# Order of the scan's parameters, the adaLN blocks, the routing groups and the final norm's scalings in a hybrid decoder block

## The chip, the cores and the metric

The kernel runs on one core of a Trainium2 chip. The metric is the device time of one execution in microseconds, as the median of several runs. The engines are TensorE (PE: matmul and transposes), VectorE (DVE), ScalarE (ACT), GpSimd (POOL) and SyncE (SP, which here only issues transfers); each runs its own instructions in program order and waits for the others at semaphores. Sixteen DMA engines move data for all of them.

## What is computed

One layer of a decoder block on x of 1024 tokens by 1024 channels, all float32, batch 1. Cut to what matters:

```python
sh1, sc1, gt1, sh2, sc2, gt2 = jnp.split(silu(c) @ w_ada + b_ada, 6, axis=-1)
xn = modulate(rmsnorm(h, norm1_g), sh1, sc1)
z_a, z_u, z_v = columns of xn @ w_in
y_a = s5_branch(z_a, ...)         # 32 groups x 64 complex states, diagonal scan over the tokens, GLU
y_b = sgu_branch(z_u, z_v, ...)   # gating with 128 x 128 causal mixing
g_a, g_b = halves of sigmoid(xn @ w_gate + b_gate)
h = h + gt1 * ((g_a * (y_a @ w_branch_a) + g_b * (y_b @ w_branch_b)) @ w_out)
xn2 = modulate(rmsnorm(h, norm2_g), sh2, sc2)
h = h + gt2 * hierarchical_moe(xn2, ...)   # top 1 of 4 groups, then top 2 of its 8 SwiGLU experts
return rmsnorm(h, norm_f_g)
```

The scan needs, for each of its 32 x 64 states, exp, cosine and sine of the parameters, powers of them, and from these tables of 128 x 128. Each token goes to two of 32 experts; each expert has two weights of 1024 x 512 and one of 512 x 1024, 201 MB in all.

## The kernel before

Tokens lie in eight tiles of 128 (NJ = 8), channels in eight blocks of 128 (KD = 8). A float32 product is made of three matmuls on split operands, high by high, low by high, high by low (`mm3`, L112 to L114).

**Prologue, to 33 us.** ScalarE squares the eight tiles of x and sums them (`square`, L558), VectorE makes the reciprocal roots of four tiles at a time (`norm_scale(h)`) and scales them, TensorE transposes them by halves of four tiles (`norm_turn(h, act)`, L572; copies out by ScalarE, or half by VectorE). `mod_block(b)` sums a quarter of the conditioning projection on TensorE (L586), copies the sums on ScalarE (`wide`), transposes them (L592) and adds the bias on VectorE. `xn_block(b)` applies shift and scale to two channel blocks and splits them. Then come the z_a products of four token tiles, two channel blocks at a time, with `xn_block(b + 1)` and `mod_block(b + 2)` between them.

`ssm_setup` is a generator that makes the scan's parameters, mostly on GpSimd with 128x16 operands; each `next(setup)` runs it to its next `yield`. Its inputs pass through three small transposes on TensorE (`prow`, L361) and one copy on ScalarE (`par`). Its rest goes to a list of side generators, of which one step is taken for each unit of products that TensorE is given. The products of the token mixer follow, unit by unit, with the transposes of the scan's tables (L524, L545) at fixed units.

**Out-projection and routing, some 560 to 668 us.** For each token tile j there are two units (j, n) of 24 matmuls each. After unit (j, 1) the tile's norm, its transposes (L1355), its router product (L1372, sixteen matmuls), its scaled row `x2` for the experts (two ScalarE instructions and two GpSimd additions, then a store to `xrows`) follow. For two tiles at a time (GROUPS) `route` picks groups and experts on VectorE (tile `rt`), counts on TensorE (L1464 to L1467), makes one-hot rows on VectorE (`ohr`), moves them on TensorE (L1493) and scatters them to a table on GpSimd (L1507). `WAIT` says for a group after how many units its two TensorE steps are put; a group not in it has (1, 1). The scatter of the last group is put off to a list `late_rows`, which runs after the first gathers.

**Experts, 668 to 1207 us.** The experts' rows are gathered by GpSimd (`x_fetch`, L1675), TensorE transposes them (L1690) and multiplies; results are added to rows in memory by GpSimd (`y_add`, L1725). Some experts have large slots with split weights, the others small slots of 64 rows. The weights are loaded on SyncE's queue into two pools of buffers; `load_next` issues the next load of a fixed list after a given expert's step. `DRAINS` names six experts after which GpSimd gets a drain instruction. Within this part, `gf_steps` spreads the final norm's gain over the partitions.

**Tail, from some 1205 us.** Eight tiles of the result are loaded. ScalarE squares each (`sum_sq`), VectorE makes the roots for three at a time (`scales(j, n)`), multiplies each tile by root and gain (`put`), and SyncE stores it. The rows of the last expert (`hlate`) are made apart, by two 64x512 instructions, and scattered by GpSimd after all stores.

## Time and profile before

| what | value |
|---|---|
| median of three runs | 1239.01 us (1237.97 to 1239.11) |
| profiled execution | 1239.78 us |
| its span | 1238.1 us |
| mean granted clock of TensorE | 0.965 |
| busy: TensorE, VectorE, ScalarE, GpSimd | 92%, 59%, 37%, 30% of the span |

The span is the part of the execution that the profiler's records cover. A clock of 1 is 2.4 GHz and 0.5 is 1.2 GHz; a mean in between says how the stretch divides into the two. Busy shares are means over stretches with different limits, so each stretch is read for itself: first which engine is busy all the time, then what the waits of that engine end on. An instruction row gives its start, its duration (of all its repetitions together where it says x4), engine, line, what it writes and reads, and in brackets how long its engine was idle before it and what ended that.

### The profile page before, as it was taken

Reading aid. Unit: us, or ns where it says so; the run is one execution under the profiler, and the core shown is the slowest. Engines: PE = TensorE matmul, PEld = TensorE weight load, DVE = VectorE, ACT = ScalarE, POOL = GpSimd, SP = SyncE. Lnnn points to the kernel's source line nnn. Section 1 sums busy time; section 2 is a strip of 40 time slices with the busy share of each in tenths; the row PEclk is TensorE's granted clock in tenths of the full one; section 3 lists DMA queues with packets and bytes.
Section 4 is the critical chain, followed back from the end, with each engine's and each line's share of the span. In section 5 each row is a group of like instructions: output and inputs, shape, how many; then the busy total and the mean of one; then the engine's idle time right before and its main releaser. Section 6 shows DMA issues by size and latency. Waiting matters only on the chain. (4 is left out here: it accounts for less than half of the span.)

```text
span 1238.1 us, 16769 instructions
## 1 busy us (share of the span) xinstructions
PE 1133.7 (92%) x6237; PEld 872.7 (70%) x6238; DVE 735.2 (59%) x1223; ACT 463.2 (37%) x664; POOL 377.6 (30%) x477
## 2 busy tenths in 40 slices
PE   4998999999999999999995999999898999898980
PEld 4897888888878888788774776666565666665630
DVE  4614562568597555656668976666464566565616
ACT  6422233234215421034324754444342444443303
POOL 2799273533000211415565111111111111111210
PEclk9999999999999999999897999999899998999995
DMA  9711122583541155545466999999999999998986
GB/s 333 222 35 58 62 86 57 197 289 102 190 151 52 35 190 175 185 166 219 152 229 241 339 353 396 401 402 404 406 400 404 388 397 377 380 394 310 381 301 271
DMA packets 106663, 313.44 MB, mean 253 GB/s; under 512 B 21035, under 2 KB 59527, under 8 KB 91858
## 3 DMA queue, kind: packets, MB, share of 16 engines
q1 hardware_dynamic: 92520, 274.14, 58.6%
q0 software_dynamic: 9088, 20.32, 6.3%
q10 hardware_dynamic: 4970, 17.88, 3.7%
q8 instruction: 50, 0.82, 0.3%
q14 instruction: 35, 0.29, 0.1%
HBM read 287.02 MB, written 33.83 MB: 259 GB/s over the span
## 5 line engine op out<-in xcount | busy, mean ns | idle before, releaser
L87 DVE TENSOR_TENSOR ewl<-wexp,ewh 128x1024 fp32r<-128x1024 f32 x176 | 207.8, 1221 | 82.0 <-ACT ewh L108 79.8
L108 ACT ACTIVATE ewh<-wexp 128x1024 fp32r<-128x1024 f32 x176 | 174.3, 1053 | 38.8 <-DMA wexp<-in_w 36.3
L112 PE MATMUL mm<-xn,wh 128*128 128x512 f32 x320 | 127.4, 398 | 0.0
L114 PE MATMUL mm<-xn,wl 128*128 128x512 f32 x320 | 125.1, 391 | 0.0
L113 PE MATMUL mm<-xn,wh 128*128 128x512 f32 x320 | 125.0, 391 | 0.0
L87 DVE TENSOR_TENSOR wl<-wraw,wh 128x1024 fp32r<-128x1024 f32 x38 | 55.0, 1456 | 110.5 <-ACT wh L108 110.5
L1741 PE MATMUL mm<-wexp,xs 128*64 128x256 f32 x992 | 115.4, 382 | 3.9 <-DMA wexp<-in_w 3.6
L1675 POOL DMA_INDIRECT xg<-xrows,w x29 | 30.7, 1060 | 282.8 <-PE aux L1690 128.6
L113 PE MATMUL mm<-ewl,xth 128*128 128x512 f32 x256 | 103.2, 403 | 0.7 <-DVE ewl L87 0.7
L1741 PEld LDWEIGHTS mm<-wexp,xs 128*64 128x64 f32 x992 | 69.0, 137 | 48.9 <-issue 9.1
L112 PE MATMUL mm<-ewh,xth 128*128 128x512 f32 x256 | 102.3, 400 | 0.2 <-ACT xth L108 0.2
L114 PE MATMUL mm<-ewh,xtl 128*128 128x512 f32 x256 | 100.5, 393 | 0.0
L1725 POOL DMA_INDIRECT hbuf<-yo,w x28 | 52.8, 1887 | 123.1 <-DVE yo L87 109.7
L798 ACT ACTIVATE gate<-mm,vcol 128x512 f32<-128x512 f32 x32 | 22.0, 688 | 134.7 <-PE mm L114 134.7
L112 PE MATMUL mm<-ewh,w 128*128 128x512 f32 x128 | 55.9, 437 | 17.7 <-ACT ewh L108 17.7
L112 PEld LDWEIGHTS mm<-xn,wh 128*128 128x128 f32 x320 | 60.4, 189 | 13.7 <-issue 1.6
L114 PEld LDWEIGHTS mm<-xn,wl 128*128 128x128 f32 x320 | 60.2, 188 | 12.8
L113 PEld LDWEIGHTS mm<-xn,wh 128*128 128x128 f32 x320 | 60.4, 189 | 11.8
L87 DVE TENSOR_TENSOR yo<-mm,macc 128x512 f32<-128x512 f32 (+1 forms) x64 | 42.7, 686 | 41.6 <-PE mm L1741 37.5
L108 ACT ACTIVATE w<-aux 128x512 fp32r<-128x512 f32 x16 | 9.6, 597 | 140.5 <-PE aux L1709 140.5
L113 PEld LDWEIGHTS mm<-ewl,xth 128*128 128x128 f32 x256 | 48.3, 189 | 19.3 <-DVE ewl L87 10.1
L108 ACT ACTIVATE wh<-wraw 128x1024 fp32r<-128x1024 f32 x38 | 39.6, 1052 | 58.6 <-PE mm L113 29.6
(369 smaller groups left out, 2454.1 us busy)
## 6 DMA issues: line engine op xcount, KB each, us to landing
wexp<-in_w SPq DMA_DIRECT2D x76, 2048.0 KB, 25.5
wexp<-in_w SPq DMA_DIRECT2D x48, 512.0 KB, 12.0
wadr<-in_w_ada SPq DMA_DIRECT2D x32, 512.0 KB, 4.8
wexq<-in_w SPq DMA_DIRECT2D x24, 512.0 KB, 9.1
wada<-in_w_ada SPq DMA_DIRECT2D x8, 1024.0 KB, 11.2
wraw<-in_w_gate SPq DMA_DIRECT2D x16, 512.0 KB, 3.8
gate<-gate ACTq DMA_DIRECT2D x16, 512.0 KB, 2.8
gin<-gate SPq DMA_DIRECT2D x16, 512.0 KB, 3.8
```

Of the source, the lines that this page charges most:

```text
L87: eng.tensor_tensor(out=o, in0=a, in1=b, op=op)
L108: A.activation(out=hi, in_=raw, func=AF.Copy)
L112: T.matmul(out=ps, lhsT=lh, rhs=rh, start=first, stop=False)
L113: T.matmul(out=ps, lhsT=lh, rhs=rl, start=False, stop=False)
L114: T.matmul(out=ps, lhsT=ll, rhs=rh, start=False, stop=last)
L798: A.activation(out=box["g"][:, sl], in_=box[hf], func=AF.Sigmoid, bias=col("bg", 8 * s + d))
L1675: G.indirect_dma_start(out=xg, out_offset=None, in_=rows[:, :], in_offset=bass.IndirectOffsetOnAxis(ap=xi, axis=0), bounds_check=rows.shap ...
L1725: G.indirect_dma_start(out=rows[:, :], out_offset=bass.IndirectOffsetOnAxis(ap=yi, axis=0), in_=yo, in_offset=None, bounds_check=rows.shap ...
L1741: T.matmul(out=ps[sl, 0:n], lhsT=xt[:, k, HALF * h:HALF * (h + 1)], rhs=w[:, n * g:n * (g + 1)], start=(kt == 0), stop=(kt == nk - 1), til ...
```

## The change

It has seven places.

1. `ssm_setup` yields once more, at step 2, and `next(setup)` is called earlier: twice before the squares, once between `norm_scale(0)` and the eighth square, once after half 0's transposes, and once more at the end.
2. `norm_turn` takes the channel blocks that it transposes. `mod_block` is cut into `mod_sums` and `mod_cols`. `norm_turn(1, ...)` is spread around the first block's two parts, and the second block's `mod_block` and `xn_block` come after the first 48 matmuls of z_a. `wz[0].split()` comes earlier.
3. `WAIT` is {(2, 3): (2, 2), (4, 5): (2, 3)} instead of {(4, 5): (2, 2), (6,): (4, 2)}, and the scatters of group (4, 5) go to `late_rows` too.
4. The last tile's row `x2` is made by one VectorE instruction.
5. The loads after a large expert's step are written two steps earlier.
6. `DRAINS` names two experts instead of six, and `gf_steps` makes a second form of the gain (`gh`) by two GpSimd copies.
7. In the tail two tiles are finished by VectorE as before; the other six are multiplied by the gain on VectorE (`by_g`) and by the root on ScalarE (`put_scaled`). The roots are made for two, three, three and one; `hlate` takes one 128x512 instruction.

```diff
@@ -565,8 +565,8 @@
         for j in range(4 * h, 4 * h + 4):
             ts(xt[j], xt[j], rs1[:, j:j + 1], None)
-    def norm_turn(h, act):
-        for k in range(KD):
+    def norm_turn(h, ks, act):
+        for k in ks:
             ps = ps_aux()
             for i in range(4):
                 T.transpose(ps[:, i * P:(i + 1) * P], xt[4 * h + i][:, k * P:(k + 1) * P], ident)
@@ -577,24 +577,30 @@
                 act_copy(o, ps)
-    mcs = {}
-    def mod_block(b):
+    mcs, mrows = {}, {}
+    def mod_sums(b):
         mps = ps_aux()
         for k in range(KD):
             for q in range(4):
                 T.matmul(out=mps[32 * q:32 * q + 32, 0:P], lhsT=cact[:, k:k + 1].to_broadcast([P, 32]),
                          rhs=wa[b][:, k, q // 2, (q % 2) * P:(q % 2 + 1) * P],
                          start=(k == 0), stop=(k == KD - 1), tile_position=(0, 32 * q))
-        mrow = tmp("wide", [P, P], bufs=1)
-        act_copy(mrow, mps[:, 0:P])
+        mrows[b] = tmp("wide", [P, P], bufs=1)
+        act_copy(mrows[b], mps[:, 0:P])
+    def mod_cols(b):
         tps = ps_aux()
-        T.transpose(tps[:, 0:P], mrow, ident)
+        T.transpose(tps[:, 0:P], mrows[b], ident)
         mc = mcs[b] = tmp("mc", [P, 4], bufs=4)
         mcv = mc.rearrange("p (s i) -> p s i", s=2)
         tt(mcv, tps[:, 0:P].rearrange("p (s i z) -> p s i z", s=2, i=2)[:, :, :, 0],
            col("b1", 0, 16).rearrange("p (s k) -> p s k", s=2)[:, :, 2 * b:2 * b + 2], OP.add)
         stt(mc[:, 2:4], mc[:, 2:4], 1.0, col("g1", 2 * b, 2), OP.add, OP.mult)
+    def mod_block(b):
+        mod_sums(b)
+        mod_cols(b)
     xn = {}
@@ -630,7 +636,7 @@
     def ssm_setup():
         for i, _ in enumerate(ssm_params()):
-            if i in (0, 1) or i % 3 == 1:
+            if i in (0, 1, 2) or i % 3 == 1:
                 yield
         first = build_tables(0)
         for _ in range(3):
@@ -651,32 +657,46 @@
     NA = 4
     setup = ssm_setup()
-    for j in range(NJ):
+    next(setup)
+    next(setup)
+    for j in range(NJ - 1):
         square(j)
     norm_scale(0)
+    next(setup)
+    square(NJ - 1)
     norm_scale(1)
+    norm_turn(0, range(KD), True)
     next(setup)
-    norm_turn(0, True)
-    norm_turn(1, False)
-    mod_block(0)
     wz[0].split()
-    next(setup)
+    mod_sums(0)
+    norm_turn(1, range(2), True)
+    mod_cols(0)
+    norm_turn(1, range(2, 4), True)
     xn_block(0)
-    mod_block(1)
+    norm_turn(1, range(4, KD), False)
     wz[2].load()
     wz[3].load()
     load_ssm()
     acc = [ps_mm() for _ in range(NA)]
     for b in range(4):
-        next(setup)
-        if b < 3:
+        if 0 < b < 3:
             wz[b + 1].split()
             xn_block(b + 1)
+        if b:
+            next(setup)
         for i in range(2):
             for j in range(NA):
                 za_mm(acc[j], j, 2 * b + i)
+            if b == i == 0:
+                mod_block(1)
+                wz[1].split()
+                xn_block(1)
         if b < 2:
             mod_block(b + 2)
+    next(setup)
     for j in range(NA):
         za_read(j, acc[j])
     side.append(setup)
@@ -1241,7 +1261,7 @@
     LASTCUT = 12
-    DRAINS = (1, 7, 13, 19, 25, NEXP - 4)
+    DRAINS = (14, NEXP - 5)
     rest = []
     def w_load(nm, e, q=nc.sync, whole=True, later=None, small=False, key=None):
@@ -1370,10 +1390,14 @@
         lps = ps_aux()
         for k in range(KD):
             T.matmul(out=lps[:, 0:36], lhsT=ht[:, k], rhs=rk["wr"][:, k], start=(k == 0), stop=(k == KD - 1))
-        for hf in range(2):
-            hs = slice(hf * 512, (hf + 1) * 512)
-            A.activation(out=x2[:, hs], in_=x2[:, hs], func=AF.Identity, scale=r)
-            tt(x2[:, hs], x2[:, hs], rowv[3][:, hs], OP.add, G)
+        if j == NJ - 1:
+            stt(x2, x2, r, rowv[3], OP.mult, OP.add)
+        else:
+            for hf in range(2):
+                hs = slice(hf * 512, (hf + 1) * 512)
+                A.activation(out=x2[:, hs], in_=x2[:, hs], func=AF.Identity, scale=r)
+                tt(x2[:, hs], x2[:, hs], rowv[3][:, hs], OP.add, G)
         nc.scalar.dma_start(out=xrows[j * P:(j + 1) * P, :], in_=x2)
         if j == NJ - 1:
             load_next(nc.scalar, nc.gpsimd)
@@ -1386,7 +1410,7 @@
             yield from route(tiles, L)
     late_rows = []
-    WAIT = {(4, 5): (2, 2), (6,): (4, 2)}
+    WAIT = {(2, 3): (2, 2), (4, 5): (2, 3)}
     GROUPS = ((0, 1), (2, 3), (4, 5), (6, 7))
     def route(tiles, L):
@@ -1511,7 +1535,7 @@
                 scatters.append(ins_)
         for t in range(B):
             tt(cum, cum, mb[:, t], OP.add)
-        if tiles[-1] >= NJ - 2:
+        if tiles[-1] >= NJ - 4:
             late_rows.append(scatter)
         else:
             scatter()
@@ -1658,6 +1682,12 @@
             T.matmul(out=ps, lhsT=rk["onef"], rhs=hi[:, hs], start=True, stop=False)
             T.matmul(out=ps, lhsT=rk["onef"], rhs=lo[:, hs], start=False, stop=True)
             act_copy(g[:, hs], ps)
+        gh = k4("gfh", [DM])[:, 0:512]
+        gf.append(gh)
+        for h in range(2):
+            sl = slice(HALF * h, HALF * (h + 1))
+            G.tensor_copy(out=gh[sl], in_=g[sl, 512 * h:512 * (h + 1)])
         yield
     late = gf_steps()
@@ -1841,6 +1871,12 @@
             hts_[e] = hid_turn(hidt, *htp)
         else:
             hid_turn_s(hid_s, xsr[1][:, e % 2])
+    def next_loads(at):
+        for _ in loads_after.get(at // 4, []):
+            load_next()
     def after(at, nm, e, i):
@@ -1881,9 +1917,8 @@
                 G.drain()
         if at < 4:
             next(ranks, None)
-        if i == 3:
-            for _ in loads_after.get(at // 4, []):
-                load_next()
+        if i == 3 and not is_l(e):
+            next_loads(at)
         if (nm, e, i) == ("w2", NEXP - 3, 0):
             late_tiles()
         if (nm, e, i) == ("w1", NEXP - 1, 0):
@@ -1907,6 +1942,8 @@
     ranks = ranking()
     for at, (nm, e, i) in enumerate(stream):
         split_to(at, at + AHEAD)
+        if is_l(e) and i == 4 - AHEAD:
+            next_loads(at)
         if nm == "w2":
             if i == 0:
                 yps[e] = [ps_mm(), ps_mm()] if is_l(e) else ps_mm()
@@ -1941,33 +1978,56 @@
         yield
         yield from rsqrt_steps(frs[:, sl], fsq[:, sl], n)
+    def store(j):
+        nc.sync.dma_start(out=out[j * P:(j + 1) * P, :], in_=hx[j])
     def put(j):
         stt(hx[j], hx[j], frs[:, j:j + 1], gf[0], OP.mult, OP.mult)
-        nc.sync.dma_start(out=out[j * P:(j + 1) * P, :], in_=hx[j])
+        store(j)
+    byg = {0: xgs[0], 1: xgs[1]}
+    def by_g(j):
+        tt(byg.setdefault(j, hx[j]), hx[j], gf[0], OP.mult)
+    def put_scaled(j):
+        A.activation(out=hx[j], in_=byg[j], func=AF.Identity, scale=frs[:, j:j + 1])
+        store(j)
     def run(steps):
         for _ in steps:
             pass
+    for j in range(4):
+        sum_sq(j)
+    by_g(0)
+    by_g(1)
+    run(scales(0, 2))
+    put_scaled(0)
+    by_g(2)
+    by_g(3)
+    sum_sq(4)
+    put_scaled(1)
+    sum_sq(5)
+    run(scales(2, 3))
+    put(4)
+    put_scaled(2)
     tt(lt["h"], lt["h"], yos[NEXP - 1][:, 0:512], OP.add)
-    for j in range(NJ):
-        sum_sq(j)
+    sum_sq(6)
+    sum_sq(7)
+    by_g(5)
+    by_g(6)
     A.activation(out=dump[:, 0:512], in_=lt["h"], func=AF.Square, accum_out=fsq[:, NJ:NJ + 1])
     sps = ps_aux()
     T.matmul(out=sps[:, 0:1], lhsT=lt["both"], rhs=fsq[:, NJ:NJ + 1], start=True, stop=True)
-    run(scales(0, 3))
-    for j in range(3):
-        put(j)
-    run(scales(3, 3))
-    for j in range(3, 6):
-        put(j)
-    V.tensor_copy(out=fsq[:, NJ:NJ + 1], in_=sps[:, 0:1])
-    run(scales(6, 3))
-    put(6)
+    put_scaled(3)
+    run(scales(5, 3))
+    put_scaled(5)
     put(7)
-    for g in range(2):
-        sl = slice(HALF * g, HALF * (g + 1))
-        stt(lt["h"][sl], lt["h"][sl], frs[sl, NJ:NJ + 1], gf[0][sl, 512 * g:512 * (g + 1)], OP.mult, OP.mult)
+    put_scaled(6)
+    run(scales(NJ, 1, sps[:, 0:1]))
+    stt(lt["h"], lt["h"], frs[:, NJ:NJ + 1], gf[1], OP.mult, OP.mult)
     G.indirect_dma_start(out=out_h[:, :], out_offset=bass.IndirectOffsetOnAxis(ap=x_index(NEXP - 1), axis=0), in_=lt["h"],
                          in_offset=None, bounds_check=2 * NT - 1, oob_is_err=False)
```

**ScalarE in the prologue.** Before, the end of the squares and of the transposes' copies (`aux_301` is half 1's seventh block) reads as follows; `wide` are the sums of an adaLN block, `wh` the high part of a weight, `xn` the split input, `par` the scan's parameters:

```order
L105 ACTIVATE xht_137<-aux_301 128x512
L105 ACTIVATE wide_346<-aux_313 128x128
L108 ACTIVATE wh_353<-wraw_109 128x1024
L615 ACTIVATE xn_68_383<-xht_131,mc_350 128x1024
L615 ACTIVATE xn_68_383<-xht_132,mc_350 128x1024
L105 ACTIVATE wide_424<-aux_391 128x128
L105 ACTIVATE par<-aux_448 128x48
L108 ACTIVATE wh_493<-wraw_114 128x1024
L615 ACTIVATE xn_68_383<-xht_133,mc_428 128x1024
L615 ACTIVATE xn_68_383<-xht_134,mc_428 128x1024
```

After the change the copy of `par` stands between the squares of the seventh and the eighth tile:

```order
L558 ACTIVATE sqs_199,ssq_129<-x_96 128x1024
L558 ACTIVATE sqs_201,ssq_129<-x_97 128x1024
L105 ACTIVATE par<-aux_223 128x48
L558 ACTIVATE sqs_229,ssq_129<-x_98 128x1024
L105 ACTIVATE xht_131<-aux_250 128x512
```

and half 1's copies (`xht`) stand between the first block's parts, with the second `wide` behind the first `xn` (L621 was L615):

```order
L108 ACTIVATE wh_337<-wraw_109 128x1024
L105 ACTIVATE wide_374<-aux_341 128x128
L105 ACTIVATE xht_131<-aux_376 128x512
L105 ACTIVATE xht_132<-aux_382 128x512
L105 ACTIVATE xht_133<-aux_393 128x512
L105 ACTIVATE xht_134<-aux_399 128x512
L621 ACTIVATE xn_65_405<-xht_131,mc_390 128x1024
L621 ACTIVATE xn_65_405<-xht_132,mc_390 128x1024
L105 ACTIVATE xht_135<-aux_413 128x512
L105 ACTIVATE xht_137<-aux_425 128x512
L105 ACTIVATE wide_498<-aux_465 128x128
L108 ACTIVATE wh_505<-wraw_114 128x1024
```

What moved: `par` forward by eighteen places, and half 1's copies behind the first `wide`.

**TensorE behind tile 5's products.** Before, the counting group of (2, 3) follows the last product of unit (5, 1) (`mm_5104`); `rt_4968` is that group's routing tile:

```order
L113 MATMUL mm_5104<-wo_4432,mh_4838 128x512
L114 MATMUL mm_5104<-wo_4431,ml_4839 128x512
L1464 LDWEIGHTS before
L1464 MATMUL aux_5143<-rt_4968,before 128x32
L1467 LDWEIGHTS ones
L1467 MATMUL aux_5143<-cum,ones 128x32
```

and the rest of that group stands ahead of tile 4's router product (L1372) and the first product of tile 6:

```order
L1467 LDWEIGHTS ones
L1467 MATMUL aux_5143<-cum,ones 128x32
L1372 MATMUL aux_5171<-rk_2032,ht_4942 128x36 x8
L1355 MATMUL aux_5185<-ident,h_4842 128x128 x4
L112 MATMUL mm_5204<-wo_4100,mh_5005 128x512
```

After, the router product (now L1392) and the transposes (now L1375) follow tile 5's products directly:

```order
L113 MATMUL mm_5104<-wo_4432,mh_4838 128x512
L114 MATMUL mm_5104<-wo_4431,ml_4839 128x512
L1392 MATMUL aux_5141<-rk_2032,ht_4942 128x36 x8
L1375 MATMUL aux_5155<-ident,h_4842 128x128 x4
L112 MATMUL mm_5174<-wo_4100,mh_5005 128x512
```

and the counting group (now L1488 and L1491) stands behind twelve products of tile 6:

```order
L114 MATMUL mm_5174<-wo_4100,ml_5006 128x512
L1488 LDWEIGHTS before
L1488 MATMUL aux_5189<-rt_4968,before 128x32
L1491 LDWEIGHTS ones
L1491 MATMUL aux_5189<-cum,ones 128x32
```

The group moved behind the router product and twelve products of other work.

**ScalarE in the tail.** Before, the eight squares, of which the order prints four and four, and that of `hlate` are the last work:

```order
L1700 ACTIVATE w_747_5610<-mm_9072 128x256
L105 ACTIVATE hts_6031<-aux_9121 128x256
L1936 ACTIVATE dump_9136,nrm<-tail_9077 128x1024 x4
L1936 ACTIVATE dump_9136,nrm<-tail_9078 128x1024 x4
L1955 ACTIVATE dump_9136,nrm<-hlate_9034 128x512
```

After, scalings (L1995) stand among the squares (L1973); the rows begin with that of tile 1, the second of three ahead of the last tile's square:

```order
L1995 ACTIVATE tail_9073<-xg_5603,nrm 128x1024
L1973 ACTIVATE dump_9132,nrm<-tail_9074 128x1024
L1995 ACTIVATE tail_9073<-tail_9073,nrm 128x1024
L1973 ACTIVATE dump_9132,nrm<-tail_9074 128x1024 x2
L2021 ACTIVATE dump_9132,nrm<-hlate_9030 128x512
L1995 ACTIVATE tail_9073<-tail_9073,nrm 128x1024
L1995 ACTIVATE tail_9074<-tail_9074,nrm 128x1024 x2
```

Three scalings now stand ahead of the last tile's square, and three behind the square of `hlate`.

## Rows read from the trace of the kernel before

**Rows 1.** Stretches: us, busy us (instructions) of each engine, clock, DMA share, GB/s

```profile
core 0: us, PE busy (x) PEld busy (x) DVE busy (x) ACT busy (x) POOL busy (x), PEclk, DMA share, GB/s
600.00:640.00 40.00, 35.05 (x187) 29.71 (x185) 33.14 (x134) 10.67 (x24) 20.27 (x22) 0.91 0.57 194
640.00:680.00 40.00, 26.56 (x125) 21.13 (x124) 27.23 (x94) 16.31 (x26) 22.12 (x23) 0.75 0.70 256
760.00:1120.00 360.00, 338.60 (x1788) 231.65 (x1788) 218.40 (x235) 156.85 (x193) 65.35 (x44) 0.97 1.01 396
```

**Rows 2.** TensorE's waits: us in total, times, longest

```profile
PE aux L545 <- DVE w L90: 4.4, 1, 4.4
PE aux L524 <- DVE sbr L87: 1.1, 1, 1.1
```

**Rows 3.** TensorE's timeline, 103 to 110 us: start, duration, line, tiles

```profile
103.59 1.97 PE L545 MATMUL aux<-ident,w 128*128 128x128 f32 x8 [4.35 <-DVE w L90]
...
105.79 0.63 PE L113 MATMUL mm<-xn,wh 128*128 128x512 f32 x1
106.21 0.63 PE L114 MATMUL mm<-xn,wl 128*128 128x512 f32 x1
...
109.11 0.39 PE L113 MATMUL mm<-xn,wh 128*128 128x512 f32 x1
109.34 0.39 PE L114 MATMUL mm<-xn,wl 128*128 128x512 f32 x1
```

**Rows 4.** GpSimd's timeline, 33 to 42 us

```profile
33.05 0.66 POOL L94 TENSOR_SCALAR par<-par 128x16 f32<-128x16 f32 x1 [18.95 <-ACT par L105]
...
39.61 1.14 POOL L87 TENSOR_TENSOR sp<-sp 128x16 f32<-128x16 f32 x1
...
41.18 0.22 POOL L87 TENSOR_TENSOR sp<-sp 128x16 f32<-128x16 f32 x1
```

**Rows 5.** Timeline of ScalarE, then of TensorE, ahead of the first products

```profile
16.88 1.06 ACT L558 ACTIVATE sqs<-x 128x1024 f32<-128x1024 f32 x1 [0.62 <-DMA x<-in_x]
...
32.11 0.33 PE L592 MATMUL aux<-ident,wide 128*128 128x128 f32 x1 [1.19 <-ACT wide L105]
```

**Rows 6.** TensorE's timeline, 605 to 642 us, around the routing groups

```profile
608.44 0.18 PE L1464 MATMUL aux<-rt,before 128*128 128x32 bf16 x1 [2.62 <-DVE rt L87]
...
608.57 3.46 PE L1372 MATMUL aux<-rk,ht 128*128 128x36 f32 x16
...
620.83 1.42 PE L1372 MATMUL aux<-rk,ht 128*128 128x36 f32 x12
...
637.93 1.43 PE L1493 MATMUL aux<-ohr 128*128 128x64 f32 x8 [1.57 <-DVE ohr L94]
...
640.36 0.63 PE L112 MATMUL mm<-wo,mh 128*128 128x512 f32 x1
```

**Rows 7.** VectorE's timeline: the same three routing steps of three groups

```profile
605.97 0.42 DVE L87 TENSOR_TENSOR rt<-rt 128x8 f32<-128x8 f32 x3
...
624.01 4.26 DVE L87 TENSOR_TENSOR rt<-rt 128x8 f32<-128x8 f32 x1
...
654.30 1.20 DVE L87 TENSOR_TENSOR rt<-rt 128x8 f32<-128x8 f32 x3
```

**Rows 8.** GpSimd's timeline, late scatters and expert 3's gather

```profile
672.82 0.99 POOL L1507 DMA_INDIRECT table<-rk,rt  x1 [0.30 <-issue]
...
683.02 1.04 POOL L1675 DMA_INDIRECT xg<-xrows,w  x1 [6.87 <-PE aux L1690]
```

**Rows 9.** Timelines of ScalarE, VectorE and GpSimd in the tail

```profile
1218.59 1.06 ACT L1936 ACTIVATE dump<-tail 128x1024 f32<-128x1024 f32 x1 [0.88 <-DMA tail<-hbuf]
...
1221.17 3.68 DVE L90 SCALAR_TENSOR_TENSOR tail<-tail,nrm,gf 128x1024 f32<-128x1024 f32 x3
...
1227.25 2.48 DVE L90 SCALAR_TENSOR_TENSOR tail<-tail,nrm,gf 128x1024 f32<-128x1024 f32 x2
...
1233.40 1.03 POOL L1971 DMA_INDIRECT out<-hlate,w  x1 [26.47 <-SPq L1978]
```

## The prediction

> **What bounds the kernel now.** I read the table of stretches first, then TensorE's waits, then the timelines around each wait. In the table [rows 1] the reader is to see three kinds of stretch. Up to 600 us the waits of TensorE, below, are the exceptions; from 600 to 680 it is busy for only 35.05 and 26.56 of 40 us, at a granted clock of 0.91 and 0.75, with DMA at 0.57 and 0.70; from 760 to 1120 DMA stands at 1.01 with 396 GB/s, while TensorE has 338.60 of 360 us. So a microsecond saved ahead of 680 is worth something only if the experts' weight loads start earlier too. They do so far as the profile tells: with DMA at 0.57 and 0.70 between 600 and 680 the loads there wait for buffers, which TensorE and VectorE free, and those events move forward with the products. After 1200 the tail is a chain of its own.
>
> **Scan parameters first.** TensorE waits once 4.4 us for the table `w` of the scan and once 1.1 us for `sbr` [rows 2]. After the 4.35 us the eight transposes take 1.97 us [rows 3]; the following products stand 0.42 us apart (105.79 to 106.21) and four of them pass before the spacing is 0.23 again (109.11 to 109.34): four times 0.2, 0.8 us. At full clock I take the transposes at half, about 1.0 us. So the place costs 4.35 + 1.1 + 1.0 + 0.8 = 7.2 us. The tables are late because GpSimd's chain of parameters begins only at 33.05, after 18.95 us of idling for `par` [rows 4]. The change puts the three transposes of `prow` first on TensorE and the copy of `par` on ScalarE ahead of the eighth square, where ScalarE sits 0.62 us for the last tile of x [rows 5] and the copy is a 128x48 tile. GpSimd then starts at about 16.5, that is 16.5 us earlier; the tables are also asked for one unit earlier (some 5.5 us by the spacing of 24 products of 0.23 us). 16.5 - 5.5 leaves 11 us against a lateness of 4.35, so both waits should vanish: **7.2 us**, all on TensorE's path. Bounds: 0 if something else on that chain is late (the rival below), 7.2 otherwise.
>
> What can slow this chain is VectorE: GpSimd's product of 128x16 takes 1.14 us at 39.61 and 0.22 us at 41.18 [rows 4], the long one beside VectorE's 128x1024 products. In its new place it runs beside the scaling of x and a chain of fourteen tiny VectorE instructions. The Trainium skill ("SBUF — State Buffer", section "Who interferes with whom") calls the port pair of VectorE and GpSimd an exclusive lock that a loser waits out for a whole instruction; it speaks against this edit, since by it the fourteen could each wait for one 0.22 us instruction, 3 us in all. [rows 4] and [rows 7] agree with it in both directions. By that sentence the next term would be -2.5 instead of +0.5.
>
> **adaLN blocks between transposes and products.** Half 1's last transposes, the second block's sums and its normalised copy move behind the first products. ScalarE is the late one here (TensorE waits 1.19 us for its `wide` at 32.11 [rows 5]). ScalarE keeps all its work, and the first half-block's copy still has to come before the first product, so I place the first product at about 32.4 (32.65 before) and the end of the first 48 about 0.5 us earlier: **0.5 us**, bounds -2 (fourteen VectorE instructions held up by GpSimd at 0.22 us each, partly hidden) and +2 (both blocks' 1.19 us waits gone).
>
> **Routing.** Now the group (2,3)'s counting products (L1464) stand directly behind tile 5's products and TensorE waits 2.62 us for VectorE's `rt`; then L1372 takes 3.46 us instead of 1.87, and transposes and products behind it are slow too [rows 6]. The one-hot group L1493 of (4,5) waits 1.57 us at 637.93, and behind it products take 0.63 us instead of 0.39, which is the picture of [rows 3]. The change moves the first behind L1372, L1355 and twelve products (1.87 + 12 x 0.23 = 4.6 us of other work for a wait of 2.62), and the second by six products (1.4 us for 1.57). Idle: 2.62 + 1.57 = 4.2. Slow clock: 3.46 - 1.87 = 1.6, some seven slots of 0.2 behind the first wait and eight behind the second, 3.0, and for the transposes an estimate of 0.4: 5.0. Together 9.2 us if nothing new waits. I take off 2.2: the second cover is short by 0.2, and VectorE's three 128x8 steps, 0.42 us alone, took 4.48 us at 624.01 beside GpSimd's 128x512 additions and scatters [rows 7]; after the change the scatters of (2,3) fall beside other steps, and one new wait of about 1 us with its slow products costs as much as that. **7.0 us**, bounds 2 (two new waits of the size of 2.62 with their slow products) and 9.2.
>
> (4,5)'s scatters join the late ones: eight instead of four, 0.99 us and 0.30 of issue each, 1.3 together, ahead of the gather that starts at 683.02 after 6.87 us of idling for TensorE [rows 8]. 4 x 1.3 = 5.2 is under 6.87, so they cost **0**. In the queue of software DMA one late scatter now waits also for a weight load that GpSimd issues just before; the gather has some 1.7 us of cover for it.
>
> **Last tile's norm.** GpSimd's two additions go, and VectorE does one 128x1024 instruction instead, 1.24 us by the tail's [rows 9]. While those additions ran, VectorE's three 128x8 steps took 1.20 at 654.30 instead of 0.42 [rows 7], and a pair of the same steps ahead of them I take to have lost 1.0. 0.8 + 1.0 - 1.24 on the routing chain is +0.6: **0.5 us**, bounds -1.24 (the additions cost nothing there) and +2.
>
> **Loads, drains, extra copies.** The large experts' loads are written two steps earlier but wait for the same split: 0. Four drains fewer: GpSimd idles for TensorE ahead of each gather, as at 683.02, so 0. The two 64x512 copies of `gf` run before the third last expert's row addition, with GpSimd idle: 0, at worst 1.
>
> **Tail.** VectorE does eight scalings at 1.24 us; its last pair ends at 1229.73 and the closing scatter, which waits for all stores, starts at 1233.40 [rows 9]. After: ScalarE takes six scalings, each at the 1.06 us of its square of the same tile, and VectorE multiplies these tiles by `gf` beforehand. The last tile's square ends at 1219.7 with 0.88 of idling ahead; three scalings now lie among the squares, which puts it at 1222.0. VectorE, with two multiplications of 1.24 behind the square of tile 6, comes to its last chain for tiles 5 to 7 at about 1222.9; that chain takes 2.2 us (2.4 with a copy, from 1224.85 to 1227.25), and two scalings of 1.06 behind it put the last store at 1227.2 to 1227.4 instead of 1229.7: **2.4 us**, bounds 0 (ScalarE's queue as late as VectorE's was) and 4 (no waits between the two engines).
>
> **Sum.** 7.2 + 0.5 + 7.0 + 0.5 + 2.4 = 17.6. The profiled execution took 1239.78 (span 1238.1, 1.7 around it): 1222.2. The median of the three runs is 0.8 lower, so **1222** for the median.
>
> **Rivals.** (a) *The weight stream does not start earlier.* If bytes and not buffers bound it already before 680, the 15.2 us ahead of it are partly lost: with half, 1239.0 - 7.6 - 2.4 = 1229; with none 1236.6. Against it: DMA at 0.57 and 0.70 ahead of 680. For it: 1.01 from 760 on. (b) *Routing's new waits eat its gain and adaLN loses*: 7.2 + 2 + 0.5 + 2.4 - 2 = 10.1, 1229. It decides where (2,3)'s L1493 meets VectorE's chain. (c) *The tables are not earlier*, because the loads of the scan's second matrices, which are not moved, or GpSimd under VectorE hold the chain: 7.2 lost, 1229. (d) *Slower*: the stream holds its time as in (a) and the eight late scatters, now inside the first experts' loads instead of at 640, push it by 4 x 1.3 = 5.2: 1239.0 + 5.2 - 2.4 = 1241.8. It decides once the scatters' end passes the gather's 683.02 and the gain ahead is under 2.8. (e) *The change does little that TensorE sees* (all waits reappear one place later): about 1238.
>
> **Chances.** Forecast (1216 to 1226) 0.58; (a) 0.14, (b) 0.10 and (c) 0.08, all between 1226 and 1237; (d) 0.05; (e) 0.05. A measurement of this kernel tells about 0.2%, 2.5 us, from no change. Faster 0.88, same 0.06, slower 0.06. Leaving out (d), (e) and the worse half of (a), some 0.15, the range ends at 1233; it begins at 1215, with the upper bounds of routing and of tail and adaLN (2.2 + 1.6 + 1.5 above the sum) and 2 us for a stream that gains more.
>
> **What would show it.** Right: GpSimd's chain starts near 16.5; no wait of L545 and L524; granted clock over 0.96 in the 40 us ahead of the last out-projection product, where 0.91 stood; first expert product some 15 us earlier; last store some 2 us nearer to the first tail square. Wrong: a wait of over 1 us at the new places of L1464 and L1493; the gather of expert 3 released by a scatter; DMA share near 1 ahead of the first expert.

## The result, and the profile after

The changed kernel takes 1230.56 us (median of 8 runs, 1226.66 to 1233.73), the kernel before 1238.08 in its 8 runs: a ratio of 0.9937, with a 95% interval of 0.9926 to 0.9949. It is 7.8 us faster by that ratio. The forecast was 1222, some 17 us faster: the direction holds and the time lies in the range, but less than half of the gain came.

The profiled execution took 1230.78 us, span 1229.0 (before 1239.78 and 1238.1). The stretches that answer to [rows 1], with the same columns:

```profile
600.00:640.00 40.00, 37.70 (x204) 31.21 (x203) 29.13 (x138) 10.58 (x24) 19.89 (x22) 0.96 0.64 222
640.00:680.00 40.00, 27.23 (x133) 21.35 (x132) 31.53 (x97) 18.61 (x28) 20.04 (x22) 0.79 0.72 268
760.00:1120.00 360.00, 339.47 (x1813) 232.88 (x1813) 215.56 (x233) 152.63 (x188) 65.75 (x44) 0.96 1.01 395
```

The routing stretch is near what the forecast said (a clock over 0.96): 0.96 instead of 0.91, TensorE busy for 2.65 us more of the 40. TensorE's waits from 83 to 160 us, which answer to [rows 2]:

```profile
PE mm L114 <- DVE wl L87: 3.4, 1, 3.4
PE aux L733 <- ACT tab L105: 0.6, 1, 0.6
```

The waits for `w` and `sbr` are gone, as forecast. But a wait stands there that the kernel before did not have: a product (L114) waits for `wl`, the low part of a gate weight.

To see where the 9 us between the two profiled executions come from, number TensorE's float32 products from the first one on and subtract each one's start from that of the same number before:

| product | start before, us | shift after, us | what lies ahead of it |
|---|---|---|---|
| 1st | 32.65 | -2.98 | first block |
| 25th | 41.35 | +1.36 | adaLN blocks 1 and 2 |
| 241st | 105.21 | -3.56 | L545, where 4.35 us of waiting stood |
| 337th | 133.79 | +0.21 | the new wait |
| 2065th | 594.19 | -0.30 | the rest of the mixer, the out-projection of tiles 0 to 4 |
| last of the out-projection | 647.50 | -6.07 | routing |
| first of an expert | 668.36 | -6.90 | last tile's norm and routing |

Of the 7.7 us of prologue and tables 0.3 are left at the 2065th product, routing gave 5.8 (6.07 less 0.30), the last tile's norm 0.8. From the first expert to the end another 2.2 us come in this execution (9.1 of spans less 6.90), of which 0.2 are the tail's (below). The rest is not the change's: in the ten other kernels below 0.8 to 3.4 us come in that part, whatever their edits, and the profiled execution of the kernel before lies 1.7 us above its median.

### The profile page after: what moved, and what is told of

Its sections match the earlier page's. It is cut to its first block, busy times and chain, and to the rows that moved or that the text cites. A ratio compares the mean times of both kernels' runs of the same rounds, so it can differ in the third digit from the quotient of the medians.

```text
span 1229.0 us, 16785 instructions
## 1 busy us (share of the span) xinstructions
PE 1133.8 (92%) x6237; PEld 873.2 (71%) x6238; DVE 728.7 (59%) x1231; ACT 470.0 (38%) x670; POOL 379.8 (31%) x477
## 5 line engine op out<-in xcount | busy, mean ns | idle before, releaser
L87 DVE TENSOR_TENSOR ewl<-wexp,ewh 128x1024 fp32r<-128x1024 f32 x176 | 207.8, 1221 | 79.0 <-ACT ewh L108 77.4
L114 PE MATMUL mm<-xn,wl 128*128 128x512 f32 x320 | 125.6, 392 | 3.4 <-DVE wl L87 3.4
L114 PE MATMUL mm<-ewh,xtl 128*128 128x512 f32 x256 | 100.7, 393 | 0.0
L114 PEld LDWEIGHTS mm<-xn,wl 128*128 128x128 f32 x320 | 60.5, 189 | 16.6 <-DVE wl L87 3.8
L113 PE MATMUL mm<-ewl,w 128*128 128x512 f32 x128 | 55.3, 432 | 6.0 <-DVE ewl L87 6.0
```

The costliest lines, as they stand in the source:

```text
L87: eng.tensor_tensor(out=o, in0=a, in1=b, op=op)
L113: T.matmul(out=ps, lhsT=lh, rhs=rl, start=False, stop=False)
L114: T.matmul(out=ps, lhsT=ll, rhs=rh, start=False, stop=last)
```

## Where the tables' 7.2 us went

TensorE's timeline around the new wait:

```profile
114.54 0.40 PE L113 MATMUL mm<-xn,wh 128*128 128x512 f32 x1
118.31 0.50 PE L114 MATMUL mm<-xn,wl 128*128 128x512 f32 x1 [3.37 <-DVE wl L87]
118.64 0.40 PE L112 MATMUL mm<-xn,wh 128*128 128x512 f32 x1
...
119.69 0.63 PE L112 MATMUL mm<-xn,wh 128*128 128x512 f32 x1
120.12 0.63 PE L113 MATMUL mm<-xn,wh 128*128 128x512 f32 x1
```

The product stands still for 3.37 us, and behind it eight products last 0.59 or 0.63 us and stand 0.38 to 0.43 apart (119.69 to 120.12) before the spacing is 0.23 again: the picture of [rows 3] at another place. The granted clock is 0.50 from 118.9 to 122.3 us. With eight times 0.2 it costs 3.37 + 1.6, 5.0 us; the second new wait (L733, 0.6 us) makes it 5.6. ScalarE and VectorE at that time:

```profile
107.89 1.06 ACT L108 ACTIVATE wh<-wraw 128x1024 fp32r<-128x1024 f32 x1
...
103.52 1.76 DVE L87 TENSOR_TENSOR w<-pp,pr 128x512 f32<-128x512 f32 x1 [3.21 <-POOL tab L87]
105.21 3.01 DVE L87 TENSOR_TENSOR sbr<-pp,pr 128x512 f32<-128x512 f32 x2
108.15 3.01 DVE L87 TENSOR_TENSOR sbr<-sbr,w 128x512 f32<-128x512 f32 x2
112.34 2.37 DVE L87 TENSOR_TENSOR w<-pp,pr 128x512 f32<-128x512 f32 x2 [1.18 <-POOL tab L87]
114.63 1.28 DVE L87 TENSOR_TENSOR tab<-pp,pr 128x512 f32<-128x512 f32 x2
115.83 1.28 DVE L87 TENSOR_TENSOR tab<-tab,w 128x512 f32<-128x512 f32 x2
117.04 1.22 DVE L87 TENSOR_TENSOR wl<-wraw,wh 128x1024 fp32r<-128x1024 f32 x1
```

The reader is to see an order. The high part of the weight (`wh`) is there at 108.95, so `wl` could be made from then on. VectorE makes it at 117.04, behind the table steps of the six rows above it, two of which wait for GpSimd (3.21 and 1.18). These table steps stand ahead of `wl` because the setup now runs one step ahead of the products. In VectorE's row of the kernel before, the third weight's split (`wl_1174`) comes first and the same table steps behind it:

```order
L87 TENSOR_TENSOR wl_1174<-wraw_1095,wh_1173 128x1024
L87 TENSOR_TENSOR w_138_1181<-pp_194,pr_195 128x512
L87 TENSOR_TENSOR w_139_1182<-pp_194,pr_195 128x512
```

In the changed kernel twelve such steps lie between the second split (`wl_1104`) and the third (`wl_1202`); the last of them:

```order
L87 TENSOR_TENSOR w_138_1165<-pp_140,pr_141 128x512
L87 TENSOR_TENSOR tab_1146<-pp_140,pr_141 128x512 x2
L87 TENSOR_TENSOR tab_1146<-tab_1146,w_137_1164 128x512
L87 TENSOR_TENSOR tab_1146<-tab_1146,w_138_1165 128x512
L87 TENSOR_TENSOR wl_1202<-wraw_1099,wh_1201 128x1024
```

That is an explanation by the trace alone. Two kernels, their combination and one part alone test it.

**e1_no_extra_step.** The last early step is taken back.

```diff
         if b < 2:
             mod_block(b + 2)
-    next(setup)
     for j in range(NA):
         za_read(j, acc[j])
```

> The changed kernel without the last of the early steps of the scan's setup (the one behind the z_a products), so that the tables are asked for at the same units as before, while GpSimd's parameters still come first. Theory A (in the changed kernel VectorE's table steps, which wait for GpSimd, stand ahead of the weight split `wl` in its queue; that split is what TensorE waits 3.37 us for at 118.31): the wait and the slow products behind it vanish and L545's wait does not come back; 5.3 us less than the changed kernel's 1230.6, about 1225, a ratio near 0.990 to the kernel before. Theory B (that weight itself comes late, or TensorE has simply caught up with it): the wait stays, within 1 us of 1230.6, ratio 0.994.

Measured: 1224.75 us, ratio 0.9895 (0.9872 to 0.9917); no wait of TensorE over its whole stretch from 83 to 160 us, neither for `wl` nor for `w`. At the 337th product it is 6.38 us ahead of the kernel before, 6.6 us ahead of the changed one. Counted from the 25th product on, where the two differ by 0.5 already, it gains 7.2 us and the changed kernel 1.2: the step costs 6.1 us, a little more than the 5.6 read above. Theory A holds, with its size.

**e2_old_adaln_place.** The parameters stay first, half 1's transposes and the blocks go back.

```diff
     norm_turn(0, range(KD), True)
     next(setup)
+    norm_turn(1, range(KD), False)
+    mod_block(0)
     wz[0].split()
-    mod_sums(0)
-    norm_turn(1, range(2), True)
-    mod_cols(0)
-    norm_turn(1, range(2, 4), True)
     xn_block(0)
-    norm_turn(1, range(4, KD), False)
+    mod_block(1)
...
     for b in range(4):
-        if 0 < b < 3:
+        if b:
+            next(setup)
+        if b < 3:
             wz[b + 1].split()
             xn_block(b + 1)
-        if b:
-            next(setup)
         for i in range(2):
             for j in range(NA):
                 za_mm(acc[j], j, 2 * b + i)
-            if b == i == 0:
-                mod_block(1)
-                wz[1].split()
-                xn_block(1)
```

> The changed kernel with half 1's transposes and the first two adaLN blocks back in their old places ahead of the products; the scan's parameters still first. The 48th product came at 51.39 in the changed kernel and at 49.99 before. Theory A (the wait for `wl` at 118 hangs on GpSimd's and VectorE's chain and not on TensorE's start): TensorE is 1.4 us earlier at the 48th product and waits 1.4 us longer for `wl`; the end is within 1 us of 1230.6. Theory B (it hangs on TensorE's own pace): 1.4 us less, 1229.2. A third possibility, that the new place of the blocks gains and another edit loses the 1.4 us: 1231 to 1233.

Measured: 1230.05 us, ratio 0.9927 (0.9908 to 0.9946). The 25th product comes 1.43 us earlier than in the changed kernel (shift -0.07 instead of +1.36), and the wait is there with another length:

```profile
117.31 0.50 PE L114 MATMUL mm<-xn,wl 128*128 128x512 f32 x1 [3.81 <-DVE wl L87]
```

It grows by 0.44 us, not by 1.4, since `wl` itself comes 1.0 us earlier, and at the 337th product 1.0 us of the 1.43 is kept (-0.78 against +0.21). The times can't tell that from nothing. What is shown is that the wait stays when the blocks go back: their place is not its cause.

**e3_both.** Both edits.

> Both edits of the two kernels beside it. Theory A: without the wait for `wl` the earlier start of the products is kept: 5.3 + 1.4 = 6.7 us less than the changed kernel, about 1224, ratio 0.989. Theory B: 1229 to 1230.

Measured: 1223.27 us, ratio 0.9873 (0.9856 to 0.989), the lowest time of this study: clearly faster than e2_old_adaln_place, but its interval overlaps that of e1_no_extra_step. TensorE is 7.60 us ahead at the 337th product and 13.37 at the first expert.

**e7_parameters_only.** The kernel before with the parameters first (the edits of `ssm_setup` and of `next(setup)` as in e3_both) and nothing else.

> The kernel before with the scan's parameters first and the tables asked for at the units of before, nothing else. Theory A (the term of 7.2 us was right in size and was lost only to the order in VectorE's queue): no wait of L545 and L524, TensorE 6.5 to 7.2 us early at 163 us, and 5.5 to 7.2 us less at the end, ratio 0.9942 to 0.9956. Rival (the gain needs the routing edits to reach the end): the shift is there at 560 us and under 3 us of it is left at the first expert's products.

Measured: 1229.33 us, ratio 0.9938 (0.9918 to 0.9957), no wait of TensorE from 83 to 160 us, and 6.9 us of shift at the 337th product, 7.2 counted from the 25th. So the term of 7.2 us had the right size, and this edit alone is worth as much as the whole change. The shift reaches the first expert (9.6 us there, with a routing stretch that is 2.1 us shorter in this execution without any edit to it).

## The other parts

**adaLN blocks.** The first product comes 2.98 us earlier, but the third waits for VectorE's `xn`:

```profile
19.66 4.25 PE L572 MATMUL aux<-ident,x 128*128 128x128 f32 x21
23.85 1.95 PE L586 MATMUL aux<-wada,cact 128*32 128x128 f32 x64
25.73 1.09 PE L572 MATMUL aux<-ident,x 128*128 128x128 f32 x8
26.66 0.27 PE L594 MATMUL aux<-ident,wide 128*128 128x128 f32 x1
26.77 2.78 PE L572 MATMUL aux<-ident,x 128*128 128x128 f32 x24
29.67 0.63 PE L112 MATMUL mm<-wh,xn 128*128 128x512 f32 x1
30.14 0.41 PE L113 MATMUL mm<-wl,xn 128*128 128x512 f32 x1
31.78 0.63 PE L114 MATMUL mm<-wh,xn 128*128 128x512 f32 x1 [1.23 <-DVE xn L87]
```

The 25th product is the first behind all that was moved, and it comes later: +1.36 in the changed kernel, +0.84 in e1_no_extra_step. Only a part of this is the place. Half 0's last transpose, ahead of all that was moved, starts at 22.64 us in the kernel before. From it to the 25th product 19.07 and 19.06 us pass in the changed kernel and in e1_no_extra_step, and 18.46 to 18.57 in the five kernels with the parameters first and the blocks in the old place (e2, e3, e6, e7, e9). So the place costs 0.6 us: the waits of 0.40 and 1.19 us for `wide` are gone, and waits for `xn` came.

The rest is the start of that last transpose itself: 23.64 and 23.13 us with the new place, but 22.26 to 23.63 in the five with the old one, though TensorE's order up to there is one and the same in all of them. The traces show why. The first of the 32 transposes starts at 15.2 to 15.9 us, and they stand 0.213 us apart until they pass to 0.109. In all twelve traces that happens, within 0.1 us, where the first record of TensorE's granted clock begins, at the full level: at 21.64 us before, 23.34 in the changed kernel, 22.98 in e1, 22.23 in e2, 21.32 in e3. (A table of stretches reads 1.00 ahead of it as well, since no lower level is recorded there; but 0.213 is also the spacing of L545's eight transposes of [rows 3], at a granted clock of 0.50.) The programs of e3_both and e9_tail_spread are the same up to the tail, and in them the record begins at 21.32 and 23.37. So this difference belongs to the execution and not to the edit.

**e10_half1_copies** asks whether ScalarE's copies for half 1 hold the place up. Its expectation puts these transposes at 2.8 us in the old place; that was misread, they have the same pace in both. e1_no_extra_step with

```diff
-    norm_turn(1, range(2), True)
+    norm_turn(1, range(2), False)
     mod_cols(0)
-    norm_turn(1, range(2, 4), True)
+    norm_turn(1, range(2, 4), False)
```

> The kernel e1_no_extra_step with half 1's first four transposed blocks copied by ScalarE and VectorE in turn, as before, instead of ScalarE alone; the new place of the adaLN blocks stays. Its 24th product stood 0.84 us later than in the kernel before, and half 1's transposes took 3.7 us of TensorE instead of 2.8. Theory A (ScalarE's copies alone slow them): the 24th product 0.7 to 0.9 us earlier than in e1_no_extra_step, the end about 1224. Rival (the place itself costs, by VectorE's `xn` behind the first two products): no change at the 24th product, 1224.75.

Measured: 1223.52 us, ratio 0.9883 (0.9864 to 0.9901), which can't be told from e1_no_extra_step. The transposes of half 1 are no faster:

```profile
25.32 1.09 PE L572 MATMUL aux<-ident,x 128*128 128x128 f32 x8
26.36 2.81 PE L572 MATMUL aux<-ident,x 128*128 128x128 f32 x24
```

But the 25th product follows 18.60 us after the start of half 0's last transpose instead of 19.06, almost as early as in the old place. So some 0.5 of the 0.6 us of the place are ScalarE's and VectorE's shares of the copies, in one execution; the times are too coarse to confirm it.

**e4_routing_only.** The kernel before with

```diff
-    WAIT = {(4, 5): (2, 2), (6,): (4, 2)}
+    WAIT = {(2, 3): (2, 2), (4, 5): (2, 3)}
...
-        if tiles[-1] >= NJ - 2:
+        if tiles[-1] >= NJ - 4:
             late_rows.append(scatter)
```

> The kernel before with the routing edits alone: the two entries of WAIT, and group (4, 5)'s scatters among the late ones. Theory A (routing is where the changed kernel's gain comes from; TensorE is 6.05 us earlier at the first expert): 5 to 6.5 us less than the kernel before, ratio 0.995 to 0.996, and L1464 at its new places with no wait over 1 us. Rival (routing's gain needs the last tile's norm or the drains beside it): under 3 us.

Measured: 1235.02 us, ratio 0.9974 (0.9959 to 0.9988), 3.2 us less by the ratio, 4.2 by the medians, with TensorE 7.0 us ahead at the first expert in the profiled execution, which was the fastest of the six. The times lie between the two theories, the trace above both; and it holds two new waits, 0.93 us for ScalarE's `ht` and 1.15 of L1464 for `rt`, of which theory A excluded the second. TensorE's rows in the changed kernel, which answer to [rows 6]:

```profile
605.37 1.87 PE L1392 MATMUL aux<-rk,ht 128*128 128x36 f32 x16
...
610.28 0.19 PE L1488 MATMUL aux<-rt,before 128*128 128x32 bf16 x1
...
614.80 1.98 PE L1392 MATMUL aux<-rk,ht 128*128 128x36 f32 x16 [1.01 <-ACT ht L105]
...
617.49 0.63 PE L112 MATMUL mm<-wo,mh 128*128 128x512 f32 x1
617.92 0.63 PE L113 MATMUL mm<-wo,mh 128*128 128x512 f32 x1
...
634.85 1.32 PE L1517 MATMUL aux<-ohr 128*128 128x64 f32 x7 [0.62 <-DVE ohr L94]
```

The 2.62 us are gone without a rest and the router product is back at 1.87; the 1.57 became 0.62; one new wait of 1.01 for ScalarE's `ht` stands at 614.80. Such a wait of about 1 us with its slow products is what the forecast took off 2.2 for, and they are there: the router product takes 1.98, and from 617.25 on the granted clock is 0.50 for 3.4 us and eight products take 1.6 us more together. Of the 9.2 us of the forecast's full gain that leaves 9.2 - 1.01 - 0.1 - 1.6 - 0.62 = 5.9, against 5.8 measured. In e4_routing_only the waits of 0.93 and 1.15 have no slow products behind them, and the gain from the 2065th product to the last of the out-projection is 6.6. In the nine kernels with the edit it is 5.7 to 7.0; in the two without it, e7 and e8, 2.1 and 0.7 us come there by themselves. VectorE's three steps of [rows 7] took 0.42, 0.49 and 0.42 us in the groups at 605.24, 624.49 and 648.15, where 0.42, 4.48 and 1.20 stood:

```profile
605.24 0.42 DVE L87 TENSOR_TENSOR rt<-rt 128x8 f32<-128x8 f32 x3
...
624.49 0.49 DVE L87 TENSOR_TENSOR rt<-rt 128x8 f32<-128x8 f32 x3
```

**e5_routing_two_drains and e6_both_six_drains** ask for the drains: e4_routing_only with two drains, and e3_both with six (one line each).

> The routing edits alone, as in the run e4_routing_only, and the two drains instead of six. There TensorE was 7.0 us early at the first expert, and the end only 4.2 us by the medians (8.9 us in the profiled execution). Theory A (the drains hold GpSimd's row additions or gathers in part of the executions): about 1232, ratio 0.994. Theory B (drains cost nothing; the difference is the scatter of the experts' part): within 1 us of 1235, ratio 0.9974.

Measured: 1230.84 us, ratio 0.9951 (0.9934 to 0.9968).

> The kernel e3_both with the six drains of before. Theory A (drains cost): 2 to 3 us more than its 1223.3, about 1226, ratio 0.9893. Theory B (they cost nothing): 1223 to 1224, ratio 0.9873.

Measured: 1223.71 us, ratio 0.9884 (0.9865 to 0.9903). The pairs are 0.9974 and 0.9951, 0.9884 and 0.9873. In both pairs the intervals overlap; two drains instead of six may be worth up to 3 us or nothing. This is inconclusive. It also says how far the times know routing: 3.2 us by one kernel and 6.1 by the other, against 7.0 forecast.

**Late scatters.** Eight of them, and the gather behind, in the changed kernel:

```profile
671.23 0.98 POOL L1531 DMA_INDIRECT table<-rk,rt  x1 [0.33 <-DMA wexp<-in_w]
672.52 1.21 POOL L1531 DMA_INDIRECT table<-rk,rt  x1 [0.30 <-issue]
676.90 1.04 POOL L1705 DMA_INDIRECT xg<-xrows,w  x1 [3.17 <-PE aux L1720]
```

The gather still waits for TensorE, now for 3.17 us where 6.87 stood [rows 8], and the scatter that waits for a weight load waits 0.33. They cost nothing, as priced.

**Last tile's norm.** Between the last out-projection product and the first expert's lie 19.98 to 20.21 us in the seven kernels with the edit (20.03 in the changed one; e1, e2, e3, e6, e9, e10) and 20.78 to 20.93 in the five without (20.86 before; e4, e5, e7, e8). It is worth 0.8 us; 0.5 was forecast.

**e8_tail_only.** The kernel before with the changed kernel's tail and `gf_steps`.

> The kernel before with the tail's edits alone (and the second form of the gain that they need). Theory A (the last three stores leave within 2.3 us of each other and their transfers take the gain back): from the first square of the tail to the closing scatter 24.3 to 24.7 us instead of 24.87, at most 0.6 us less at the end, ratio 0.9995 to 1. Theory B (the forecast's 2.4 us are there and something else in the changed kernel hides them): 22.5 us for that stretch, 2.4 us less, ratio 0.998.

Measured: 1237.02 us, ratio 0.9997 (0.9988 to 1.0007); 24.65 us from the first tail square to the closing scatter, where 24.87 stood and 24.64 in the changed kernel. (The kernels with the old tail have 24.39 to 24.87, so even these 0.2 us are not clear.) Theory A's numbers hold. SyncE's issues of the last stores, before:

```profile
1228.57 0.33 SPq L1946 DMA_DIRECT2D out<-tail  x1
1229.76 0.33 SPq L1946 DMA_DIRECT2D out<-tail  x1
```

and after, with the two scalings that ScalarE ends on and the closing scatter:

```profile
1216.06 2.19 ACT L1995 ACTIVATE tail<-tail,nrm 128x1024 f32<-128x1024 f32 x2 [1.09 <-DVE nrm L90]
...
1217.24 0.33 SPq L1982 DMA_DIRECT2D out<-tail  x1
1217.66 1.44 SPq L1982 DMA_DIRECT2D out<-tail  x1
1219.19 0.38 SPq L1982 DMA_DIRECT2D out<-tail  x1
...
1224.24 1.04 POOL L2031 DMA_INDIRECT out<-hlate,w  x1 [26.75 <-SPq L2038]
```

The last tile is ready at 1218.25, 18.65 us after the first square (1199.60), where it was 21.20 before (1229.73 less 1208.53): the 2.4 us of the forecast are there in ScalarE and VectorE. But three stores come at once. The second issue takes 1.44 us instead of 0.33, so the last store, ready at 1218.25, is issued at 1219.19; and from the end of the last issue to the scatter it is 4.67 us instead of 3.31 (1230.09 to 1233.40), behind three stores that were issued within 2 us instead of two.

**e9_tail_spread.** e3_both with another order of the tail's second half.

```diff
     run(scales(2, 3))
     put(4)
+    sum_sq(6)
+    sum_sq(7)
     put_scaled(2)
-    tt(lt["h"], lt["h"], yos[NEXP - 1][:, 0:512], OP.add)
-    sum_sq(6)
-    sum_sq(7)
     by_g(5)
-    by_g(6)
+    tt(lt["h"], lt["h"], yos[NEXP - 1][:, 0:512], OP.add)
...
     put_scaled(5)
+    put(6)
     put(7)
-    put_scaled(6)
```

> The kernel e3_both with another order in the tail: the squares of tiles 6 and 7 ahead of tile 2's scaling on ScalarE, tile 6 finished by VectorE, so that VectorE's last chain for tiles 5 to 7 starts when tile 7's square ends and tiles 2, 3, 5, 6, 7 are stored one after another. Theory A (the last three stores start late and together, 1217.2 to 1219.6 us in the changed kernel, while DMA stood at 0.34 to 0.58 of its time ahead of them): from the first tail square to the closing scatter 22.4 to 23 us instead of 23.9 to 24.8, and about 1.5 us less than e3_both at the end, near 1221.7. Rival (the tail is bound by its 8 MB and not by the order): 24.5 us as in the others and 1223.3.

Measured: 1224.73 us, ratio 0.9891 (0.9873 to 0.9909). The stretch is 23.55 us, below the 23.91 to 25.22 of the other kernels with this tail but not the 22.4 to 23 of theory A, and the end shows nothing. One issue still stalls:

```profile
1211.26 0.33 SPq L1973 DMA_DIRECT2D out<-tail  x1
...
1212.60 1.73 SPq L1973 DMA_DIRECT2D out<-tail  x1
```

So the order explains a part of it at most. Here too three stores were issued within 1.4 us (1211.26 to 1212.60). That the stores hold each other up is a reading of the traces that no run confirms.

## Why the prediction was wrong, point by point

- **Scan parameters: the step that failed.** GpSimd's chain started at 16.76 (16.5 forecast) and both waits vanished. The mistake is in the clause "the tables are also asked for one unit earlier". I used it only to reduce the slack, 16.5 - 5.5 = 11 us. I did not count what that unit's step puts into VectorE's queue: twelve table instructions of 128x512, two of which wait for GpSimd, ahead of a weight split that TensorE needs. Their price was 3.37 us of waiting, 1.6 of slow products and a second wait of 0.6, 5.6 of the 7.2 removed (6.1 by the products of e1_no_extra_step). e1_no_extra_step takes out just that step and gets 5.8 us back by the medians (5.2 by the ratios); e7_parameters_only shows the term itself at 6.9, or 7.2 from the 25th product on. Rival (c) had about the size (7.2 lost) but the wrong reason: the tables came in time for TensorE, and it was a weight that they delayed.
- **adaLN: wrong sign by the traces.** A gain of 0.5 was forecast; at the 25th product the pairs with and without it lose 1.2 and 1.4 us (e1 against e3, the changed kernel against e2). Of this the place explains 0.6, and the rest is when half 0's transposes end, which changes from execution to execution with the moment of the full clock. The times of neither pair show a difference. All of it is inside the bounds. I reckoned with the first product, which did come earlier, and not with the 25th, which is the first that shows the whole rearrangement.
- **The Trainium skill's lock** ("SBUF — State Buffer", "Who interferes with whom"): by it I reckoned that tiny VectorE instructions beside GpSimd could lose 3 us in the prologue. VectorE's second chain of fourteen started at 17.82 and its scaling at 20.08, 2.26 us later, where 18.06 and 20.24 stood, 2.18 us apart: the chain loses next to nothing. The one that waits here is GpSimd, whose first instruction takes 1.14 us beside VectorE's scaling where 0.66 stood. The same section of the Trainium skill also has a VectorE instruction with two inputs in SBUF contend with a GpSimd instruction that reads SBUF. The routing rows above agree: the three steps took 4.48 us beside GpSimd's additions and 0.49 us without them.
- **Routing: right mechanism, size 5.8 in the trace** (7.0 forecast; 5.7 to 7.0 in nine traces), 3.2 and 6.1 by the times. One new wait of 1.01 with eight slow products came, as assumed; the 2.2 taken off for it and for the short cover should have been 3.3.
- **Late scatters and last tile's norm: right** (0 and 0.8). The loads' 0 was not tested by itself. The drains: not settled.
- **Tail: the term was mis-sized by leaving out a resource.** The 2.4 us between engines are there; at most 0.2 reach the end. I followed the last store neither through SyncE's queue, where the issue ahead of it took 1.44 us, nor to its landing, 4.67 us behind its issue instead of 3.31. What makes these two longer stays open.
- **The weight stream:** rival (a) did not happen. DMA stood at 0.64 and 0.72 ahead of the experts, and in every profiled execution the span fell by at least what TensorE had gained at the first expert (e3_both: 13.4 us there, 16.2 of span, 15.7 by its ratio).
- **The sum.** By the trace 0.3 for prologue and tables, 5.8, 0.8 and 0.2: 7.1 instead of 17.6. The profiled execution had 9.0, the medians have 7.5. (The forecast's own arithmetic, 1222.2 less 0.8, gives 1221 and not 1222.)

## What to carry to other kernels

When a generator of side work is advanced by a step, print what that step's instructions stand ahead of on each in-order engine: the gain was lost to a weight split queued behind table steps that themselves waited for GpSimd. Follow a change to the first instruction behind everything that was moved, and a store through its queue to its landing. Before a difference of a microsecond in one trace is given to an edit, look whether TensorE's clock rose or fell at another moment. Where a wait is removed, look for the next consumer of the same engine.

## What the runs showed of the hardware

- Behind a wait TensorE's clock can fall. Behind 3.37 us (the changed kernel) and 3.81 us (e2_old_adaln_place) the granted clock was 0.50, or 1.2 GHz, for 3.4 us, and eight products stood 0.43 us apart instead of 0.23: 1.6 us, the same for both. Behind the 1.01 us at 614.80 it fell as well, and behind 0.93 and 1.15 us in e4_routing_only it did not. So a wait of about 1 us can cost 1 us or 2.6.
- At the start of the program 128x128 transposes stood 0.213 us apart, and 0.109 from the moment at which the record of the granted clock begins at the full level. That moment lay between 20.64 and 23.37 us in the twelve traces, and 2 us apart in two kernels that are the same program up to the tail.
- Store issues of 512 KB on SyncE's queue took 0.33 us in most cases, but 1.44 (the changed kernel, 1217.66) and 1.73 us (e9_tail_spread, 1212.60) when others had left within a microsecond. That alone does not make them slow: in the changed kernel the one at 1211.55 followed another by 0.42 us, as that at 1217.66 did, and took 0.38.
- Executions of one kernel differ more than I had reckoned with: the changed one from 1226.66 to 1233.73; and the routing stretch of a kernel without any edit to it was 2.1 us shorter in its profiled execution (e7_parameters_only), the whole of e8_tail_only 5 us, with a timed ratio of 1.000. Terms under 2 us can be read from single profiled executions only where several kernels agree, as for the last tile's norm.
